# One row of a modulation product moved from TensorE to VectorE, and the first loads of a decoder layer put in another order

## The chip, the cores and the metric

The kernel runs on one core of a Trainium2 chip. The metric is the device time of one execution in microseconds (us). Beside the time of every run there is one profiled execution of the kernel before, and all rows below come from it.

A core has five engines that work side by side: TensorE (PE, matrix products; its weight loads are listed as PEld), VectorE (DVE), ScalarE (ACT), GpSimd (POOL) and SyncE (SP, which here only issues DMA transfers). Each engine runs its own instructions in a fixed order and waits on semaphores of the others. ACT can issue transfers too.

## The reference, cut to what matters

The reference is one decoder layer on 256 tokens of width 2048. A vector `c` gives six modulation rows; the rest is a norm, a mixer of three head groups, a residual add, a second norm, a mixture of 32 experts, and a last norm:

```
mod = (silu(c) @ ada_w + ada_b)[:, None, :]
sh1, sc1, g1, sh2, sc2, g2 = jnp.split(mod, 6, axis=-1)
h = rmsnorm(x, norm1_g) * (1.0 + sc1) + sh1
x = x + g1 * hybrid_mixer(h, w_in, conv_w, a_log, dt_bias, dn_norm_g, sinks, w_out)
h = rmsnorm(x, norm2_g) * (1.0 + sc2) + sh2
x = x + g2 * hierarchical_moe(h, rg_w, rg_b, re_w, re_b, w_gate, w_up, w_down)
return rmsnorm(x, final_norm_g)
```

`ada_w` is 2048 x 12288. Each of the six rows is a product of one vector of 2048 with a 2048 x 2048 block, so each costs 16 tiles of 128 x 2048 (1 MB each). All is float32; the large products split a number into two float32r parts.

## The kernel before, in words

Weights pass through ring slots of 128 x 2048 floats (1 MB). A `Stream` holds the queue of loads; `st.grow(...)` hands it slots, `pump()` issues a load for each free slot on SP's queue, and `done()` frees a slot once its tile was used. The first 90 tiles come from `early`: slices of sh1 and sc1 (`ada_tile`, the tiles named `prow`), slices of the input projection, then paired columns of it and the output projection `w_out`. The other four rows come from `ada_w`, 64 tiles: g1 (i = 0), sh2 (1), sc2 (2) and g2 (3). After that come the experts.

At the start the kernel reads `c`, `x` (four tiles `xt`, 512 KB each), six small pieces of norm1_g and ada_b (`crow`), and `w_bb` (`wbr`). It squares x on ACT (`ssq`, then `rs`, a square root, a reciprocal), spreads the result over the columns (`rd`, `rb`), turns the modulation of the first 256 columns into `mod` (`modulate`), and forms the normed, modulated input `hx` (`input_rows`), with which the projections `w` start. This is repeated for each of six slices of the 2048 columns.

`split` cuts a weight tile into a high part (a cast on ACT) and a low part (a subtraction, on VectorE or on GpSimd by turns); its tiles are `stg`.

`row_tile(i, kt)` takes tile kt of row i of `ada_w`. There are two forms. `on_pe` issues four TensorE matmuls (32 x 512) per tile that add up in PSUM (`prow`). `on_dve` keeps a 128 x 2048 sum `racc` in SBUF: two VectorE instructions per tile (128 x 1024 each: a multiplication for kt = 0, a multiply-add after that), and at kt = 15 four matmuls with the column `onec`, which add the partitions of `racc` up. Before, only i = 2 (sc2) took `on_dve`.

The mixer runs the DeltaNet (`delta`) on many short steps between TensorE and VectorE: `vtok`, `Um`, `ktok`, `Sm`, `ob`, `qk`. Between its steps `tick()` puts tiles of the attention groups, of the remaining input projection and of the rows. Then `wout_part` does the output projection in 4 parts and a second round of 4: products into two PSUM banks `w` from a ring of three, then on VectorE a multiplication with g1 (`g1s`) and an addition to x1. Behind each of the first four parts stand two g2 tiles (kt = 8 to 15); kt = 0 to 7 stand in `fill` before.

The order on each engine is not the program's order alone: the kernel is built with a scheduler that places instructions by a model of their durations, so an edit can move instructions elsewhere. A transfer takes one of eight semaphores in turn, over all queues together; the issue waits until the transfer that had that semaphore before has landed.

## Time and profile before

| what | value |
|---|---|
| median of 3 runs | 1624.28 us (1623.28 to 1625.85) |
| the profiled execution's own time | 1624.69 us |
| its span in the profile | 1622.9 us |
| mean granted TensorE clock | 0.98 |
| busy: PE, PEld | 1521.0 us (94%), 926.3 us (57%) |
| busy: DVE, ACT, POOL | 732.8 us (45%), 400.4 us (25%), 184.0 us (11%) |

The span is the time from the first to the last recorded instruction; the 1.8 us between it and the time lie around it. Busy times are sums over the whole span, and the span has stages with different limits, so the table alone doesn't say what an edit is worth.

### The profile page before, as it was taken

Reading aid. Unit: us, or ns where it says so; the run is one execution under the profiler, and the core shown is the slowest. Engines: PE = TensorE matmul, PEld = TensorE weight load, DVE = VectorE, ACT = ScalarE, POOL = GpSimd, SP = SyncE. Lnnn points to the kernel's source line nnn. Section 1 sums busy time; section 2 is a strip of 40 time slices with the busy share of each in tenths; the row PEclk is TensorE's granted clock in tenths of the full one; section 3 lists DMA queues with packets and bytes.
Section 4 is the critical chain, followed back from the end, with each engine's and each line's share of the span. In section 5 each row is a group of like instructions: output and inputs, shape, how many; then the busy total and the mean of one; then the engine's idle time right before and its main releaser. Section 6 shows DMA issues by size and latency. Waiting matters only on the chain. (4 is left out here: it accounts for less than half of the span.)

```text
span 1622.9 us, 23431 instructions
## 1 busy us (share of the span) xinstructions
PE 1521.0 (94%) x9852; PEld 926.3 (57%) x9852; DVE 732.8 (45%) x1201; ACT 400.4 (25%) x691; POOL 184.0 (11%) x103
## 2 busy tenths in 40 slices
PE   5999999999999999899999999999999999999895
PEld 3778877678776677445445445455445435445433
DVE  3544587487624544333443443344235225325325
ACT  4333366444443344120110110111011101101103
POOL 1111223234333241000000000000000000000001
PEclk8999999999999999899999999999999999999998
DMA  9977654888857374799999999999999999999995
GB/s 377 408 300 290 216 224 178 349 316 320 312 216 291 144 305 180 281 410 420 392 420 420 421 421 420 421 420 420 420 421 421 420 421 421 421 420 420 422 420 223
DMA packets 81412, 573.74 MB, mean 354 GB/s; under 512 B 9740, under 2 KB 10100, under 8 KB 12312
## 3 DMA queue, kind: packets, MB, share of 16 engines
q1 hardware_dynamic: 81272, 572.20, 87.4%
q8 instruction: 79, 1.29, 0.3%
q14 instruction: 29, 0.24, 0.0%
q10 hardware_dynamic: 32, 0.01, 0.0%
HBM read 570.07 MB, written 2.10 MB: 353 GB/s over the span
## 5 line engine op out<-in xcount | busy, mean ns | idle before, releaser
L67 PE MATMUL u<-ring,xg 128*64 128x512 f32 x2048 | 483.7, 602 | 7.5 <-DMA ring<-in_expert_gu_dram 7.3
L67 PEld LDWEIGHTS u<-ring,xg 128*64 128x64 f32 x2048 | 134.4, 136 | 235.7 <-issue 190.7
L67 PE MATMUL d<-ring,hidT 128*64 128x256 f32 x2048 | 239.1, 384 | 12.0 <-DMA ring<-in_expert_dn_dram 8.6
L67 PE MATMUL w<-hx,stg 128*128 128x256 f32 x1440 | 191.0, 288 | 7.4 <-ACT hx L349 2.8
L67 PEld LDWEIGHTS d<-ring,hidT 128*64 128x64 f32 x2048 | 144.1, 137 | 93.1 <-issue 10.6
L67 PEld LDWEIGHTS w<-hx,stg 128*128 128x128 f32 x1440 | 177.9, 191 | 32.8 <-issue 10.9
L290 POOL TENSOR_TENSOR stg<-ring,stg 128x1024 fp32r<-128x1024 f32 x50 | 121.9, 2439 | 373.0 <-ACT stg L289 273.4
L289 ACT CAST stg<-ring 128x1024 fp32r<-128x1024 f32 x116 | 121.3, 1047 | 164.3 <-PE w L67 140.9
L1248 DVE TENSOR_TENSOR xt<-xt,s 128x512 f32<-128x512 f32 x120 | 82.5, 687 | 159.2 <-PE s L67 158.4
L1235 ACT CAST yh<-z 64x512 fp32r<-64x512 f32 (+1 forms) x132 | 78.8, 597 | 279.2 <-DVE z L1232 274.3
L1232 DVE SCALAR_TENSOR_TENSOR z<-d,gs,g2b 64x512 f32<-64x512 f32 (+1 forms) x132 | 95.8, 726 | 84.0 <-PE d L67 81.8
L290 DVE TENSOR_TENSOR stg<-ring,stg 128x1024 fp32r<-128x1024 f32 x66 | 91.4, 1385 | 65.2 <-ACT stg L289 65.0
L67 PE MATMUL prow<-ring,csil 128*32 128x512 f32 (+1 forms) x768 | 102.3, 565 | 13.8 <-DMA ring<-in_early_dram 13.5
L1337 POOL TENSOR_TENSOR xf<-xt,fgb 128x1024 f32<-128x1024 f32 x3 | 7.0, 2359 | 953.1 <-DVE xf L1232 953.1
L1165 DVE TENSOR_TENSOR xg<-g,sh2c 128x512 f32<-128x512 f32 x64 | 43.6, 690 | 136.8 <-PE u L67 76.2
L67 PEld LDWEIGHTS s<-yh,wt 128*128 128x128 f32 x240 | 45.4, 189 | 96.4 <-issue 60.4
L1204 ACT ACTIVATE hid<-u 64x512 f32<-64x512 f32 x32 | 18.9, 590 | 317.4 <-PE u L67 300.8
L1236 DVE TENSOR_TENSOR yl<-z,yh 64x512 fp32r<-64x512 f32 (+1 forms) x132 | 87.3, 661 | 5.1 <-ACT yh L1235 1.5
L67 PE MATMUL s<-yh,wt 128*128 128x256 f32 x240 | 75.6, 335 | 9.1 <-ACT yh L1235 5.0
L67 PE MATMUL w<-stg,hx 128*128 128x256 f32 x576 | 81.1, 291 | 0.7 <-DVE ak L271 0.7
L1205 DVE TENSOR_TENSOR hid<-hid,u 64x512 f32<-64x512 f32 x32 | 22.1, 690 | 129.8 <-ACT hid L1204 129.6
L67 PEld LDWEIGHTS w<-stg,hx 128*128 128x128 f32 x576 | 71.1, 189 | 13.2 <-issue 9.8
(396 smaller groups left out, 1590.4 us busy)
## 6 DMA issues: line engine op xcount, KB each, us to landing
ring<-in_expert_gu_dram SPq DMA_DIRECT2D x256, 1024.0 KB, 19.8
ring<-in_expert_dn_dram SPq DMA_DIRECT2D x128, 1024.0 KB, 19.8
ring<-in_early_dram SPq DMA_DIRECT2D x90, 1024.0 KB, 8.2
ring<-in_ada_w_dram SPq DMA_DIRECT2D x64, 1024.0 KB, 6.4
xt<-in_x_dram SPq DMA_DIRECT2D x8, 512.0 KB
out_dram<-xt SPq DMA_DIRECT2D x8, 256.0 KB, 3.9
fgb<-in_final_norm_g_dram SPq DMA_DIRECT2D x1, 1024.0 KB
rw<-in_router_w_dram SPq DMA_DIRECT2D x1, 320.0 KB, 5.1
```

What stands on the lines that cost most here:

```text
L67: return T.matmul(o, lhsT, rhs, start=start, stop=stop, skip_group_check=True)
L289: S.copy(hi, src)
L290: (G if nsplit[0] % GS[part] == GS[part] - 1 else V).tensor_tensor(lo, src, hi, op=ALU.subtract)
L1165: V.tensor_tensor(self.xg[:, 2 * q:2 * q + 2, 0:w], p[:, 0:2 * w].rearrange("p (k s) -> p k s", k=2), sh2c.rearrange("p n k -> p (n k)")[: ...
L1204: S.activation(hid[64:128], p[0:64], AF.Silu)
L1205: V.tensor_tensor(hid[0:64], hid[64:128], p[64:128], op=ALU.mult)
L1232: V.scalar_tensor_tensor(o.rearrange("p (n j) -> p n j", n=m), pd[q, 0:256 * m].rearrange("p (n j) -> p n j", n=m), gs[q, h, u:u + 1], g2h ...
L1235: S.copy(ys[h][q, c], o)
L1236: V.tensor_tensor(yl[h][q, c], o, ys[h][q, c], op=ALU.subtract)
L1248: V.tensor_tensor(x1[n][:, b], x1[n][:, b], p, op=ALU.add)
L1337: G.tensor_tensor(xf[n // 2][:, n % 2], x1[n], fgb[:, None, 512 * n:512 * (n + 1)].to_broadcast([P, NB, 512]), op=ALU.mult)
```

## The change

The g2 row (i = 3) takes `on_dve` as the sc2 row does. At the start, `st.grow(main, side)` (five 1 MB tiles of `early`) stands before the four x loads on SP's queue, not behind them; the six small row loads and `w_bb` are issued from ACT's queue and no longer from SP's, the small rows lie in `scratch` buffers (tag `t2`, four of them, which the squares use too), and the cast and the subtraction that make `wbb` stand ahead in the program. The layout of x (128 rows of 4 KB per tile) is the same in both kernels.

```
     cols, crows = {}, {}
     for nk, r in ((4, 4), (2, 8)):
         w = P * nk
-        rows = crows[nk] = tmp.tile([P, 2, 256], F32, name="crow", tag="ct", bufs=2).rearrange("p u t -> p (u t)")[0:3 * r, 0:w]
-        for i, row in enumerate((norm1_g[0, 0:r * w], ada_b[0, 0:r * w], ada_b[0, D:D + r * w])):
-            start_loads.append((rows[i * r:(i + 1) * r], row.rearrange("(j n) -> j n", n=w)))
+        rows = crows[nk] = scratch(w, 3 * r)
+        S.dma_start(rows[0:r], norm1_g[0, 0:r * w].rearrange("(j n) -> j n", n=w))
+        S.dma_start(rows[r:2 * r], ada_b[0, 0:r * w].rearrange("(j n) -> j n", n=w))
+        S.dma_start(rows[2 * r:3 * r], ada_b[0, D:D + r * w].rearrange("(j n) -> j n", n=w))
...
+    st.grow(*main, *side)
     for n in range(4):
         nc.sync.dma_start(x1[n], xin[n])
-    st.grow(*main, *side)
-    wbr = tmp.tile([P, 2, 384], F32, name="wbr", tag="pT").rearrange("p u s -> p (u s)")[:, 0:16 * KT]
-    for a in start_loads + [(wbr, w_bb)]:
-        nc.sync.dma_start(*a)
...
+    wbr = tmp.tile([P, 2, 384], F32, name="wbr", tag="pT").rearrange("p u s -> p (u s)")[:, 0:16 * KT]
+    S.dma_start(wbr, w_bb)
...
+    S.copy(wbb[0], wbr)
+    V.tensor_tensor(wbb[1], wbr, wbb[0], op=ALU.subtract)
...
         def f(t):
-            (on_dve if i == 2 else on_pe)(t)
+            (on_dve if i >= 2 else on_pe)(t)
...
     V.tensor_copy(rb, pt[:, 0:256])
-    S.copy(wbb[0], wbr)
-    V.tensor_tensor(wbb[1], wbr, wbb[0], op=ALU.subtract)
     use(first[3:CP])
```

How the order moves, at three places. First the start, on TensorE. `prow` are the products of the modulation slices (four 1 MB tiles are 32 matmuls), `d<-ident` are transposes of the small rows and of x, `t_225`/`t_227` is the scaled identity that carries the root of the squares, `t_244` and `t_248` are the copies of `prow` for sh1 and sc1, and `w` are the projections. Before:

```order
L180 MATMUL d<-ident,t_104 128x16
L67 MATMUL prow<-ring,csil 32x256 x40
L233 MATMUL d<-ident,crow 128x12 x4
L233 MATMUL d<-ident,crow 128x24 x2
L67 MATMUL d<-t_225,ones 128x128 x2
L67 MATMUL d<-ones,t_244 128x1 x2
L67 MATMUL d<-ones,t_248 128x1 x2
L334 MATMUL d<-ident,xt_66 128x128 x4
L67 MATMUL prow<-ring,csil 32x256 x8
L67 MATMUL w<-hx,stg 128x256 x48
L67 MATMUL prow<-ring,csil 32x256 x8
```

The same place on TensorE in the changed kernel:

```order
L181 MATMUL d<-ident,t_110 128x16
L67 MATMUL prow<-ring,csil 32x256 x32
L232 MATMUL d<-ident,t_101 128x12 x4
L232 MATMUL d<-ident,t_105 128x24 x2
L67 MATMUL d<-t_227,ones 128x128
L67 MATMUL d<-ones,t_244 128x1 x2
L337 MATMUL d<-ident,xt_66 128x128 x4
L67 MATMUL prow<-ring,csil 32x256 x6
L67 MATMUL d<-t_227,ones 128x128
L67 MATMUL d<-ones,t_248 128x1 x2
L67 MATMUL prow<-ring,csil 32x256 x10
L67 MATMUL w<-hx,stg 128x256 x36
```

One tile's eight `prow` matmuls moved from before the small transposes to behind those of x, and sixteen stand directly ahead of `w`. On ACT's queue the order at the start is now this (before, `c` alone was issued there, the squares L518 stood directly behind its activation, and the cast of `wbr` stood behind the two copies of `prow`):

```order
L241 DMA wbr<-in_w_bb_dram 128x256
L168 DMA t_99<-in_c_dram 16x128
L174 DMA t_101<-in_norm_g_dram 4x512
L175 DMA t_101<-in_ada_b_dram 4x512
L176 DMA t_101<-in_ada_b_dram 4x512
L174 DMA t_105<-in_norm_g_dram 8x256
L175 DMA t_105<-in_ada_b_dram 8x256
L176 DMA t_105<-in_ada_b_dram 8x256
L294 ACT_TABLE_LOAD
L294 CAST wbb_149<-wbr 128x256
L179 ACT_TABLE_LOAD
L179 ACTIVATE t_110<-t_99 16x128
```

The activation of `c`, on which all `prow` matmuls depend, now stands behind eight issues, a cast and a second table load.

Second, the hand-over from the second to the third slice, on TensorE (`t_881` is the copy of the last modulation row, whose four columns `d<-ones,t_881` go to VectorE for `mod`). Before:

```order
L67 MATMUL w<-hx,stg 128x256 x22
L67 MATMUL d<-ones,t_881 128x1 x4
L67 MATMUL prow<-ring,csil 32x512 x4
L67 MATMUL w<-hx,stg 128x256 x2
L67 MATMUL w<-hx,wbb_151 16x256
```

In the changed kernel:

```order
L67 MATMUL w<-hx,stg 128x256 x32
L67 MATMUL d<-ones,t_881 128x1 x3
L67 MATMUL w<-hx,stg 128x256 x12
L67 MATMUL d<-ones,t_881 128x1
L67 MATMUL prow<-ring,csil 32x512 x8
L67 MATMUL w<-hx,stg 128x256 x2
L67 MATMUL w<-hx,wbb_149 16x256
```

Behind the last `d<-ones` now stand eight `prow` matmuls, where there were four.

Third, VectorE between the end of the DeltaNet and the output projection. Before, in the second half of the DeltaNet's last unit (L907 to L909 and L914 feed TensorE, L925 adds `ob`):

```order
L914 TENSOR_TENSOR t_4993<-d,beta 128x512
L925 TENSOR_TENSOR ob<-ob,d 128x512
L907 TENSOR_TENSOR t_5007<-d,egc 128x512
L909 TENSOR_TENSOR ob<-d,egc 128x512
L908 TENSOR_TENSOR t_5007<-vtok,t_5007 128x512
L914 TENSOR_TENSOR t_5016<-d,beta 128x512
```

In the changed kernel:

```order
L915 TENSOR_TENSOR t_4977<-d,beta 128x512
L444 SCALAR_TENSOR_TENSOR racc<-ring,csil,racc 128x1024 x2
L926 TENSOR_TENSOR ob<-ob,d 128x512
L444 SCALAR_TENSOR_TENSOR racc<-ring,csil,racc 128x1024
L908 TENSOR_TENSOR t_4991<-d,egc 128x512
L444 SCALAR_TENSOR_TENSOR racc<-ring,csil,racc 128x1024
L910 TENSOR_TENSOR ob<-d,egc 128x512
L909 TENSOR_TENSOR t_4991<-vtok,t_4991 128x512
L915 TENSOR_TENSOR t_5000<-d,beta 128x512
```

Four `racc` instructions stand between the steps of the chain; twenty others stand ahead of this place, behind sc2's last product. And in the second and third part of the output projection (L975/L976 multiply the PSUM bank `w`, L976/L977 add it to x1), before:

```order
L975 TENSOR_TENSOR w<-w,g1s 128x512 x2
L976 TENSOR_TENSOR xt_5025<-xt_5025,w 128x512 x2
L290 TENSOR_TENSOR stg<-ring,stg 128x1024 x2
L975 TENSOR_TENSOR w<-w,g1s 128x512 x2
L976 TENSOR_TENSOR xt_5026<-xt_5026,w 128x512 x2
L290 TENSOR_TENSOR stg<-ring,stg 128x1024
```

In the changed kernel:

```order
L976 TENSOR_TENSOR w<-w,g1s 128x512 x2
L444 SCALAR_TENSOR_TENSOR racc<-ring,csil,racc 128x1024
L291 TENSOR_TENSOR stg<-ring,stg 128x1024
L444 SCALAR_TENSOR_TENSOR racc<-ring,csil,racc 128x1024
L977 TENSOR_TENSOR xt_5009<-xt_5009,w 128x512 x2
L291 TENSOR_TENSOR stg<-ring,stg 128x1024
L976 TENSOR_TENSOR w<-w,g1s 128x512
L444 SCALAR_TENSOR_TENSOR racc<-ring,csil,racc 128x1024 x2
L976 TENSOR_TENSOR w<-w,g1s 128x512
L977 TENSOR_TENSOR xt_5010<-xt_5010,w 128x512
```

The multiplication and the addition that free a PSUM bank are no longer neighbours. The remaining `racc` instructions stand in front of the first and behind the last of these rows.

## Rows read from the trace of the kernel before

**Rows 1.** The busy time of each engine in two stretches of the span (start:end, length, then busy us and count for PE, PEld, DVE, ACT and POOL, the granted TensorE clock as a share of full speed, the share of the DMA engines, GB/s).

```profile
0.00:690.00 690.00, 644.21 (x4558) 494.44 (x4559) 369.95 (x611) 280.58 (x486) 177.03 (x100) 0.97 0.72 277
690.00:1600.00 910.00, 869.91 (x5252) 427.44 (x5251) 350.97 (x568) 111.58 (x188) 0.00 (x0) 0.99 1.01 418
```

**Rows 2.** The timeline of the first 45 us (start, us, engine, line, operation, out<-in, shapes and count; in brackets the idle time before it and what ended it).

```profile
0.76 1.82 SPq L221 DMA_DIRECT2D xt<-in_x_dram  x4
...
9.27 0.19 ACT L518 ACTIVATION_READ_ACCUMULATOR t<-xt 128x1 f32 x1
...
10.64 1.94 PE L67 MATMUL prow<-ring,csil 128*32 128x256 f32 x16 [6.69 <-DMA ring<-in_early_dram]
...
11.21 0.48 DVE L526 TENSOR_SCALAR t<-ident,rs 128x128 f32<-128x128 f32 x2
...
18.01 1.94 PE L67 MATMUL prow<-ring,csil 128*32 128x256 f32 x16 [0.56 <-DMA ring<-in_early_dram]
...
24.08 0.63 PE L334 MATMUL d<-ident,xt 128*128 128x128 f32 x4
29.24 1.94 PE L67 MATMUL prow<-ring,csil 128*32 128x256 f32 x16 [4.53 <-DMA ring<-in_early_dram]
31.24 7.86 PE L67 MATMUL w<-hx,stg 128*128 128x256 f32 x48
...
40.72 4.47 PE L67 MATMUL w<-hx,stg 128*128 128x256 f32 x38
```

**Rows 3.** Busy times, granted clock and transfer rate of a short stretch at the start, columns as in rows 1.

```profile
30.00:40.00 10.00, 9.94 (x76) 8.27 (x68) 8.10 (x22) 4.45 (x7) 1.39 (x6) 0.72 1.02 428
```

**Rows 4.** The timeline at the hand-over from the second to the third slice, columns as in rows 2.

```profile
86.44 1.07 PE L67 MATMUL prow<-ring,csil 128*32 128x512 f32 x8
...
86.83 2.34 POOL L290 TENSOR_TENSOR stg<-ring,stg 128x1024 fp32r<-128x1024 f32 x1 [9.36 <-ACT stg L289]
86.89 2.30 DVE L324 SCALAR_TENSOR_TENSOR mod<-mod,cols 128x4 f32<-128x4 f32 x1
...
90.31 0.80 PE L67 MATMUL w<-hx,stg 128*128 128x256 f32 x2 [2.79 <-ACT hx L349]
...
91.24 1.94 PE L67 MATMUL prow<-ring,csil 128*32 128x512 f32 x8
```

**Rows 5.** The row matmuls on TensorE from 440 to 600 us: the two groups (count, ns min/median/max, first and last start), and a row of their timeline. A 512-wide matmul leaves two records, so eight are one tile; 128 of the 136 start after sc2's `racc,onec` and are g2's 16 tiles.

```profile
L67 PE MATMUL prow<-ring,csil x136: 592/592/617, 440.8 to 567.4; 128*32 128x512 f32 x136
L67 PE MATMUL prow<-racc,onec x8: 592/605/617, 455.6 to 456.0; 128*32 128x512 f32 x8
...
564.72 1.91 PE L67 MATMUL prow<-ring,csil 128*32 128x512 f32 x12
```

**Rows 6.** sc2's row on VectorE (tile `racc`): durations in ns, first and last start, and, from the groups of VectorE's lines in 310 to 437 us, the busy us and the mean.

```profile
L441 DVE SCALAR_TENSOR_TENSOR racc<-ring,csil,racc x30: 1255/1276/3402, 317.2 to 432.9; 128x1024 f32<-128x1024 f32 x30
L439 DVE TENSOR_SCALAR racc<-ring,csil x2: 741/741/741, 312.2 to 312.8; 128x1024 f32<-128x1024 f32 x2
...
L441 DVE SCALAR_TENSOR_TENSOR racc<-ring,csil,racc 128x1024 f32<-128x1024 f32 x30 | 42.4, 1453 | 4.1 <-DMA ring<-in_ada_w_dram 4.1
```

**Rows 7.** Busy times by stretch, columns as in rows 1: where sc2's row is on VectorE (310 to 437, and ten microseconds of it in which VectorE has no gap), and from sc2's last product to the end of the DeltaNet.

```profile
310.00:437.00 127.00, 122.20 (x999) 103.28 (x998) 98.29 (x135) 53.82 (x120) 49.94 (x28) 1.00 0.84 319
320.00:330.00 10.00, 7.72 (x60) 5.65 (x56) 9.92 (x15) 2.06 (x4) 4.04 (x2) 1.00 0.90 326
...
456.60:510.00 53.40, 53.40 (x397) 40.69 (x395) 18.59 (x29) 22.80 (x44) 19.10 (x9) 1.00 0.73 276
510.00:527.60 17.60, 15.39 (x96) 9.57 (x94) 7.84 (x11) 2.81 (x4) 4.44 (x4) 1.00 0.75 284
```

**Rows 8.** The timeline of VectorE and GpSimd where both work on SBUF, and the same VectorE line a little later.

```profile
495.43 2.40 POOL L938 TENSOR_TENSOR tok<-tok,dng 128x1024 f32<-128x1024 f32 x1
...
496.22 2.15 DVE L917 TENSOR_TENSOR t<-t,ekd 128x512 f32<-128x512 f32 x1
...
506.00 0.69 DVE L917 TENSOR_TENSOR t<-t,ekd 128x512 f32<-128x512 f32 x1
```

**Rows 9.** The timeline of TensorE and VectorE at the end of the DeltaNet.

```profile
514.49 2.78 PE L67 MATMUL prow<-ring,csil 128*32 128x512 f32 x22
...
519.26 0.69 DVE L914 TENSOR_TENSOR t<-d,beta 128x512 f32<-128x512 f32 x1 [0.20 <-PE d L67]
...
522.82 1.06 PE L67 MATMUL prow<-ring,csil 128*32 128x512 f32 x8
...
524.53 1.13 PE L67 MATMUL d<-t,Um 128*128 128x128 f32 x8 [0.64 <-DVE t L908]
...
525.69 0.69 DVE L914 TENSOR_TENSOR t<-d,beta 128x512 f32<-128x512 f32 x1 [1.31 <-PE d L67]
```

**Rows 10.** The timeline of the output projection around its first and second part.

```profile
547.62 1.40 DVE L975 TENSOR_TENSOR w<-w,g1s 128x512 f32<-128x512 f32 x2 [2.51 <-PE w L67]
...
548.82 1.92 PE L67 MATMUL prow<-ring,csil 128*32 128x512 f32 x16 [0.30 <-DMA ring<-in_ada_w_dram]
548.92 1.27 DVE L976 TENSOR_TENSOR xt<-xt,w 128x512 f32<-128x512 f32 x2
...
550.12 1.22 DVE L290 TENSOR_TENSOR stg<-ring,stg 128x1024 fp32r<-128x1024 f32 x1
...
551.94 0.86 PE L67 MATMUL w<-stg,aq 128*128 128x512 f32 x3
```

More of the change, by code (lines that the diff above doesn't have):

```diff
@@ L168, in hybrid_moe @@
     S.dma_start(craw, c[0].rearrange("(k p) -> k p", p=P))
-    cols, crows, start_loads = {}, {}, []
+    cols, crows = {}, {}
     for nk, r in ((4, 4), (2, 8)):
         w = P * nk
-        rows = crows[nk] = tmp.tile([P, 2, 256], F32, name="crow", tag="ct", bufs=2).rearrange("p u t -> p (u t)")[0:3 * r, 0:w]
-        for i, row in enumerate((norm1_g[0, 0:r * w], ada_b[0, 0:r * w], ada_b[0, D:D + r * w])):
-            start_loads.append((rows[i * r:(i + 1) * r], row.rearrange("(j n) -> j n", n=w)))
+        rows = crows[nk] = scratch(w, 3 * r)
+        S.dma_start(rows[0:r], norm1_g[0, 0:r * w].rearrange("(j n) -> j n", n=w))
+        S.dma_start(rows[r:2 * r], ada_b[0, 0:r * w].rearrange("(j n) -> j n", n=w))
+        S.dma_start(rows[2 * r:3 * r], ada_b[0, D:D + r * w].rearrange("(j n) -> j n", n=w))
     V.memset(csil, 0.0)
```

## The prediction

> **What bounds the kernel now.** I read the profile in this order: busy times by stretch, the waits of TensorE, then the timelines of the two regions that the change touches, and last the chain of instructions on VectorE there. The busy times [rows 1] split the span in two. From 690 us on, the DMA engines move 418 GB/s without a gap (share 1.01): the experts' weights set the pace there, and nothing of this change lies in that stretch. Up to 690 us the DMA share is 0.72 and TensorE is busy 644 of 690 us, VectorE 370: there TensorE is the bound. The expert loads follow on as ring slots come free, so a microsecond won before about 680 us should shift the whole rest by a microsecond. The change has to be worth what it takes from TensorE's line before that point, less what TensorE then waits for.
>
> **The start.** Before, x (2 MB) goes first, and the five early tiles behind it arrive 2.46 us apart (TensorE takes the first at 10.64, the fourth at 18.01) [rows 2]. With the tiles ahead of x, the first lands about 2 x 2.46 = 4.9 us earlier, at 5.7, and the fifth at 15.6; the x tiles of half a megabyte then land from 17 to 20.8. Two things follow.
>
> The squares, which ended at 9.46 before, now wait for x: two squares of 0.8 us behind the last x tile end at 22.4. From the last square to the end of the scaled identity took 11.69 - 9.27 = 2.4 us [rows 2], so it is ready at about 24.8, where before it was ready at 11.7 and waited for TensorE. Meanwhile the activation of `c` waits behind eight issues on ACT, one of which waits for the semaphore of the first early tile; with two table loads and the cast I put `csil` at 11, and four tiles of products at 1.94 us end at 18.8. They are not last; `csil` could be 5 us later without a cost. TensorE is then idle for some 6 us to 24.8, where before it was idle 4.53 us to 29.24 [rows 2].
>
> From there the second half of the spread, the modulation, the normed columns and `hx` follow. The like of it ran from the transposes of x (24.08 to 24.71) to 31.24 before [rows 2], 6.5 us, so I put the first `w` at 31.5 instead of 31.24: no gain. But before, TensorE came to `w` out of its wait at half clock: 48 matmuls took 7.86 us, 38 later ones 4.47 (0.118 each), and the granted clock of 30 to 40 us was 0.72 [rows 2, 3]. In the new order sixteen `prow` matmuls (fifth and sixth tile, both landed) stand ahead of `w`, and I take the 48 at 0.118: 5.7 us. The end of this group moves from about 40.1 to 38.2: **1.9 us gained**. If the clock rises later, little is left (0.5); if the chain to `hx` is shorter because GpSimd is elsewhere, 3.
>
> **The hand-over at 87 us.** Before, TensorE did four matmuls (1.07 us, eight records) behind the last modulation column, then was idle for 2.79 us until `hx`, and ran the next ones at half clock (1.94 for eight records) [rows 4]. On the way a VectorE instruction of 128 x 4 took 2.30 us beside a GpSimd subtraction that began 0.06 us earlier. Eight matmuls stand there now: one microsecond more cover, and as the wait shortens some of the half clock goes too. **2.0 us gained**; 0 if the schedule around it shifts the gap elsewhere, 4.6 if wait and half clock both go. The other reorderings up to 130 us move work between engines that show no wait of TensorE there; I cost them at nothing, since the ring is full and TensorE's queue covers them (where a new gap opened, it would be of this size, 1 to 3 us).
>
> **g2 off TensorE.** The 128 records are 16 tiles. A tile alone shows 1.07 us [rows 4], one and a half in a row 1.91 [rows 5]; at the middle of 1.07 and 1.27, some 1.19 each, they are 19.0 us of TensorE in all. By their places in the timeline 9.6 of it lies in 459 to 493, 4.7 in 510 to 524, 4.7 behind 548. On VectorE they become 2 instructions of 0.74 and 30 of 1.28 at the median, 1.45 at the mean with what GpSimd blocks [rows 6], 40 to 45 us, and two pieces of `onec` products come back to TensorE (1.0 us each by a tile's price).
>
> 456 to 510 us: TensorE has no gap there, VectorE is busy 18.6 us of 53.4 [rows 7]. The new order puts 20 `racc` instructions in: 2 x 0.74 + 18 x 1.28 = 24.5, or 27.6 at the mean. That makes 43 to 46 us of VectorE work, and TensorE's share falls to 53.4 - 9.6 = 43.8. So VectorE becomes as full as TensorE. Where sc2's row did this before, VectorE at 77% (98.3 of 127) went with 4.8 us of 127 lost by TensorE, but ten microseconds without a gap on VectorE (9.92) with 2.28 of 10 [rows 7]. Between these, at some 15% of 44 us, TensorE loses 6.6 of its 9.6: **3.0 us gained**, bounds 0 and 9.6.
>
> 510 to 528 us: the new order puts two plus one plus one `racc` instructions between steps of the chain that leads to the last `qk` product. From L914 at 519.26 to L914 at 525.69 took 6.4 us [rows 9]. In the new order that is about 0.6 + 2 x 1.28 + 0.6 + 1.28 + 0.6 + 1.28 + 0.6 + 0.7 + 1.0 (TensorE's product between) = 9.2: 2.8 us more, and nothing is left for TensorE in this time. Ahead of it the `prow` pieces of 510 and 514 go (3.7 us), of which some 2.9 was not needed to cover the chain. **0**, bounds -3 and +2.
>
> 548 to 568 us: 4.7 us of `prow` go. But in the second part L976 now follows L975 behind two `racc` and a split: 1.40 + 1.28 + 1.22 + 1.28 + 0.64 = 5.8 us until the first PSUM bank is free, where TensorE has twelve matmuls of some 0.24 us as cover (2.8) [rows 10]: 3.0 us idle at most. In the third part two `racc` (2.6 us) stand inside the pair, against a cover of some seven: about 2 us. With the `onec` pieces (2.0) that is 7.0 against 4.7: **2 us lost** (bounds -5 and +1).
>
> The sum is 1.9 + 2.0 + 3.0 + 0 - 2.0 = 4.9 us gained. Of the profiled execution's 1624.69 us that leaves 1619.8; the median of before is 0.4 lower than that execution, so I give 1619.4.
>
> **Two instructions on one memory.** The rows show that a VectorE instruction with two SBUF inputs is held while GpSimd works: L917 took 2.15 us beside a GpSimd instruction, 0.69 alone [rows 8]. The Trainium skill (SBUF — State Buffer, "Who interferes with whom") speaks against this change: VectorE and GpSimd share a pair of ports under an exclusive lock, and a VectorE instruction with two SBUF inputs and a GpSimd one that reads SBUF hold each other off for the whole instruction. The trace agrees, and each `racc` multiply-add is of that kind. By the rule, with GpSimd busy 19.1 of 53.4 us [rows 7], VectorE would have 43 + 19 = 62 us of work there if all of it collided, and the gain of that stretch would turn into a loss of 8; the mean of 1.45 against 1.28 says that in sc2's stretch only about a seventh was lost. So I price the rule as the far end of rival C.
>
> **The rivals.**
>
> A, the forecast above: chance 0.43, its own range 1614 to 1624.
>
> B, VectorE hides g2 altogether: TensorE has the matmuls no more and nothing else waits. Then 19.0 - 2.0 = 17.0 with the 3.9 of the first two places: 1624.7 - 20.9 - 0.4 = 1603.4. For it: VectorE's 45% and 370 of 690 us [rows 1]. Against it: the ten full microseconds of rows 7 and the written order. Chance 0.12.
>
> C, slower: `racc` ahead of the chain's and the output projection's steps. In 456 to 510 nothing is won; at the end of the DeltaNet the 2.8 us longer chain and two locks of 1.46 us (2.15 - 0.69) cost 5.8, the output projection 3.3 and two locks more, 6.2. With 3.9 won at the start, that is 8.1 lost: 1624.7 + 8.1 - 0.4 = 1632.4. It decides as soon as these stretches lose more than 7.2 us together. For it: the order on VectorE is fixed, and TensorE has no filler left between these steps. Against it: GpSimd is busy only 4.4 of 17.6 us there [rows 7]. Chance 0.20.
>
> D, nothing is won at the start and the hand-over: the wait for the squares takes the place of the wait for the tiles, and half clock stays. Then only 3.0 + 0 - 2.0 is left: 1623.3. For it: x is 16 us later, and TensorE's new idle time (6 us) is longer than the old one (4.53). Chance 0.25.
>
> **How the numbers follow.** A measurement of this kernel can tell some 0.2% from no change, 3.25 us: faster is below 1621.0, slower above 1627.5. B and four fifths of A are faster (0.12 + 0.34), and a sliver of D: 0.47. Same is the rest of A and most of D: 0.30. Slower is C and a little of D where a new gap opens at the start: 0.23. The range leaves B out (0.12) and the far half of C: 1608 to 1631.
>
> **What would show it.** Right: first `w` near 31 us at full clock; the idle time at the hand-over under 2 us; VectorE over 90% busy from 456 to 505 with TensorE short of full; TensorE waits for `t` and for `w` banks released by VectorE between 505 and 570. Wrong: first `w` clearly behind 33 us, or a wait of `prow` for `csil` behind 16 us (the start); TensorE without gaps from 456 to 570 (B); waits there of over 15 us (C).

## The result, and the profile after

The changed kernel takes 1633.49 us (median of 6 runs, 1630.71 to 1634.44); the kernel before took 1624.53 us beside it (6 runs). The ratio is 1.0051 (95%: 1.0041 to 1.0061): **slower by 0.5%**, where 1619.4 was forecast. The profiled execution took 1630.71 us, its span 1628.9. It is the fastest of the six, and its span is 6.0 us longer than that of before: the rows below account for 6.0 of the 8.3 us that the ratio gives.

The windows of the changed kernel, columns as in rows 1, answer to [rows 1, 3, 7]:

```profile
0.00:690.00 690.00, 626.10 (x4401) 495.11 (x4401) 409.56 (x642) 281.06 (x487) 179.36 (x100) 0.95 0.71 273
690.00:1600.00 910.00, 872.47 (x5245) 427.96 (x5244) 346.81 (x559) 107.09 (x178) 0.00 (x0) 0.99 1.01 418
456.60:510.00 53.40, 46.70 (x312) 41.06 (x311) 46.27 (x46) 22.60 (x44) 20.71 (x8) 0.90 0.80 315
510.00:527.60 17.60, 9.80 (x53) 8.26 (x53) 12.84 (x15) 1.17 (x2) 3.16 (x3) 0.80 0.52 180
30.00:40.00 10.00, 9.91 (x97) 8.19 (x90) 9.72 (x29) 4.90 (x8) 1.14 (x4) 1.00 1.01 420
```

TensorE has 18 us less to do up to 690 us, and is not done sooner: its idle time grew from 45.8 to 63.9 us, and its granted clock fell from 0.97 to 0.95. From 690 us on the two are nearly alike.

**Where the time went.** One and the same instruction is looked up in both timelines, and its start before is taken from its start after. Four places do: sc2's product on TensorE (455.6 before [rows 5]), the last two `t<-d,beta` of the DeltaNet (519.26 and 525.69 [rows 9]), and the last multiplication with g1, at 642.00 before:

```profile
642.00 1.39 DVE L975 TENSOR_TENSOR w<-w,g1s 128x512 f32<-128x512 f32 x2 [6.15 <-PE w L67]
```

In the changed kernel (the second of the four rows is that of 519.26 before):

```profile
451.98 1.07 PE L67 MATMUL prow<-racc,onec 128*32 128x512 f32 x8
514.51 0.69 DVE L915 TENSOR_TENSOR t<-d,beta 128x512 f32<-128x512 f32 x1 [0.71 <-PE d L67]
525.73 0.69 DVE L915 TENSOR_TENSOR t<-d,beta 128x512 f32<-128x512 f32 x1 [2.23 <-PE d L67]
648.84 1.39 DVE L976 TENSOR_TENSOR w<-w,g1s 128x512 f32<-128x512 f32 x2 [6.15 <-PE w L67]
```

So the changed kernel is 3.57 us ahead at 456, 4.75 ahead at 519, level at 526, and 6.84 behind at 642. These four shifts, called s1 to s4, are given for every experiment below. Only e2 and e3 have none: the executions that were profiled, 1928.53 and 1747.44 us, ran at a lower clock throughout, and the ratios leave them out.

The timeline at the start, at the hand-over, at one wait of TensorE in between, and at TensorE's waits in the chain and in the output projection, there with what stands ahead of them on VectorE:

```profile
24.89 0.80 PE L67 MATMUL d<-t,ones 128*128 128x128 f32 x2 [7.00 <-DVE t L529]
31.35 4.67 PE L67 MATMUL w<-hx,stg 128*128 128x256 f32 x36
...
86.32 0.17 DVE L327 SCALAR_TENSOR_TENSOR mod<-mod,cols 128x4 f32<-128x4 f32 x1
86.59 2.37 POOL L291 TENSOR_TENSOR stg<-ring,stg 128x1024 fp32r<-128x1024 f32 x1 [10.33 <-ACT stg L290]
89.29 0.74 PE L67 MATMUL w<-hx,stg 128*128 128x256 f32 x4 [1.07 <-DVE hx L353]
...
476.38 2.07 PE L67 MATMUL w<-stg,hx 128*128 128x256 f32 x8 [2.02 <-DVE stg L291]
...
515.12 3.59 DVE L444 SCALAR_TENSOR_TENSOR racc<-ring,csil,racc 128x1024 f32<-128x1024 f32 x2
516.55 1.08 POOL L943 TENSOR_TENSOR t<-ob 128x512 f32<-128x512 f32 x1 [0.90 <-PE d L67]
519.24 1.27 DVE L444 SCALAR_TENSOR_TENSOR racc<-ring,csil,racc 128x1024 f32<-128x1024 f32 x1
521.03 1.27 DVE L444 SCALAR_TENSOR_TENSOR racc<-ring,csil,racc 128x1024 f32<-128x1024 f32 x1
522.83 0.67 DVE L909 TENSOR_TENSOR t<-vtok,t 128x512 f32<-128x512 f32 x1
523.65 2.05 PE L67 MATMUL d<-t,Um 128*128 128x128 f32 x8 [5.50 <-DVE t L909]
...
542.41 2.16 DVE L291 TENSOR_TENSOR stg<-ring,stg 128x1024 fp32r<-128x1024 f32 x1 [2.17 <-ACT stg L290]
544.63 7.59 SPq L190 DMA_DIRECT2D ring<-in_ada_w_dram  x2
549.38 2.48 DVE L444 SCALAR_TENSOR_TENSOR racc<-ring,csil,racc 128x1024 f32<-128x1024 f32 x2 [3.62 <-DMA ring<-in_ada_w_dram]
551.78 1.29 DVE L976 TENSOR_TENSOR w<-w,g1s 128x512 f32<-128x512 f32 x2
554.17 1.22 DVE L291 TENSOR_TENSOR stg<-ring,stg 128x1024 fp32r<-128x1024 f32 x1
555.44 0.80 PE L67 MATMUL w<-stg,aq 128*128 128x512 f32 x1 [4.23 <-DVE stg L291]
573.36 0.73 PE L67 MATMUL w<-stg,aq 128*128 128x512 f32 x2 [1.96 <-DVE xt L977]
```

Three things are to be read here. At 523.65 the eight products of the chain have waited 5.50 us, where they waited 0.64 before [rows 9], and then take 2.05 us where they took 1.13. At 549.38 VectorE, with a g2 tile at the head of its queue, stands still for 3.62 us until that tile has landed; the split of 554.17 is queued behind, and TensorE, which needs it at 551.2, waits 4.23 us. Before, TensorE took a g2 tile at nearly the same time (548.82) and waited 0.30 [rows 10].

The tile could not land sooner. SP's queue had stood for 21.9 us until the end of VectorE's split of 542.41 freed a ring slot; the tile's load went out at 544.63 (the row holds two loads, this is the first), and VectorE could go on 4.75 us later. Before, the same load went out at 543.97. So the change did not make this tile late; it changed who waits for it.

And behind such waits the granted clock falls; 0.50 is its lower level, 1.2 GHz. Behind 476.38 and behind 555.44, in short windows:

```profile
475.00:480.00 5.00, 3.62 (x17) 3.62 (x18) 5.00 (x8) 2.49 (x11) 0.00 (x0) 0.60 0.73 249
480.00:485.00 5.00, 5.00 (x41) 4.63 (x40) 4.05 (x6) 3.60 (x6) 3.45 (x1) 0.71 0.97 381
...
555.00:560.00 5.00, 4.56 (x11) 3.59 (x12) 2.78 (x4) 0.00 (x0) 0.00 (x0) 0.50 0.85 306
```

### The profile page after: what moved, and what is told of

It reads as the page before. It is cut to its first block, busy times and chain, and to the rows that moved or that the text cites. A ratio compares the mean times of both kernels' runs of the same rounds, so it can differ in the third digit from the quotient of the medians.

```text
span 1628.9 us, 23242 instructions
## 1 busy us (share of the span) xinstructions
PE 1510.4 (93%) x9732; PEld 930.9 (57%) x9732; DVE 772.8 (47%) x1233; ACT 400.9 (25%) x692; POOL 186.3 (11%) x103
## 3 DMA queue, kind: packets, MB, share of 16 engines
q8 instruction: 78, 1.28, 0.3%
## 5 line engine op out<-in xcount | busy, mean ns | idle before, releaser
L444 DVE SCALAR_TENSOR_TENSOR racc<-ring,csil,racc 128x1024 f32<-128x1024 f32 x60 | 86.6, 1475 | 7.0 <-DMA ring<-in_ada_w_dram 7.0
L67 PE MATMUL w<-stg,hx 128*128 128x256 f32 x576 | 84.5, 299 | 2.9 <-DVE stg L291 2.0
L67 PEld LDWEIGHTS w<-stg,hx 128*128 128x128 f32 x576 | 74.6, 198 | 13.5 <-issue 8.3
```

Source lines behind the costliest of these rows:

```text
L67: return T.matmul(o, lhsT, rhs, start=start, stop=stop, skip_group_check=True)
L444: V.scalar_tensor_tensor(acc[:, c], t[:, c], csil[:, kt, 3:4], acc[:, c], op0=ALU.mult, op1=ALU.add)
```

## The experiments

Every ratio is to the kernel before, run in turn on the same chip; e13 is a single run. "Start" means the changed order of the first loads with all that belongs to it.

| label | what it is | median us | ratio (95%) | s1 | s2 | s3 | s4 |
|---|---|---|---|---|---|---|---|
| after | start, all of g2 on VectorE | 1633.49 | 1.0051 (1.0041 to 1.0061) | -3.57 | -4.75 | +0.04 | +6.84 |
| e1_start | start alone | 1621.16 | 0.9979 (0.9971 to 0.9988) | -2.86 | -2.86 | -2.85 | -3.52 |
| e2_g2 | g2 alone | 1637.0 | 1.0073 (1.0060 to 1.0086) | | | | |
| e9_xfirst | e1, x ahead of the five tiles | 1619.81 | 0.9970 (0.9959 to 0.9981) | -3.84 | -3.84 | -3.83 | -4.56 |
| e3_g2_first8 | start, tiles 0 to 7 on VectorE | 1621.54 | 0.9979 (0.9969 to 0.9990) | | | | |
| e13_first8_again | the same once more | 1623.2 | (one run) | -1.06 | -3.39 | -2.37 | -2.43 |
| e4_g2_last8 | start, tiles 8 to 15 on VectorE | 1634.4 | 1.0059 (1.0046 to 1.0072) | -1.62 | -4.73 | +0.02 | +9.75 |
| e5_chain | start, tiles 8 to 11 on VectorE | 1626.34 | 1.0010 (1.0001 to 1.0019) | -3.34 | -6.45 | -1.71 | +0.25 |
| e6_wout | start, tiles 12 to 15 on VectorE | 1632.31 | 1.0048 (1.0034 to 1.0062) | -1.39 | -1.39 | -1.38 | +8.86 |
| e7_pinned | after, tiles 8 to 15 in program order | 1633.52 | 1.0045 (1.0032 to 1.0059) | -1.41 | -3.28 | -3.27 | +11.93 |
| e12_pinned_no_pool | e7, no GpSimd splits in the output projection | 1628.4 | 1.0018 (1.0009 to 1.0027) | -2.49 | -3.84 | -3.83 | +3.82 |
| e10a_tiles | e6, tiles 12 to 15 one part later | 1623.22 | 0.9983 (0.9974 to 0.9992) | -1.12 | -1.12 | -1.11 | -0.49 |
| e10b_resident | e10a, data already in SBUF | 1622.01 | 0.9977 (0.9968 to 0.9986) | -2.48 | -2.49 | -2.48 | -2.69 |
| e14_resident_early | e6's place, data already in SBUF | 1616.71 | 0.9945 (0.9931 to 0.9958) | -0.75 | -0.76 | -0.74 | -1.68 |
| e15_swapped | e6, the g2 tiles loaded and used first | 1627.29 | 1.0013 (1.0004 to 1.0022) | -1.70 | -1.70 | -0.57 | +2.18 |
| e16_xfirst_swapped | e15, x ahead of the five tiles | 1625.82 | 1.0002 (0.9993 to 1.0011) | -4.31 | -4.31 | -3.17 | -0.45 |

e13 repeats e3 for its trace. s1 holds the start, and differs by up to 2.8 us between kernels whose start is the same, so of the other parts the steps from s1 on are read.

### The two halves of the change: e1_start, e2_g2

My theory after the result: the start wins, g2 on VectorE loses. e1 takes back g2, e2 takes back the start.

```
-            (on_dve if i >= 2 else on_pe)(t)
+            (on_dve if i == 2 else on_pe)(t)
```

> The start's edits alone; g2 stays on TensorE as before. Theory (the loss is g2's row between the steps of the DeltaNet and of the output projection; the start is a gain): the 4.5 us that the trace of the changed kernel is ahead at 300 us stay to the end, about 1620 us against 1624.5. Rival (the start is paid back later, by the ring or by the experts' loads): 1623 to 1625.

> g2 on VectorE alone; the start as before. Theory: the changed kernel without its 4.5 us at the start, 1635 to 1638 us. Rival (start and g2 don't simply add, because the new start is what makes g2's tiles late): 1624 to 1630.

The theory holds, and both times fall into their ranges: e1 is 0.2% faster (some 3.4 us), e2 0.7% slower (some 11.9). Their sum, 8.5 us slower, is the change (8.3).

### Which tiles lose: e3_g2_first8, e4_g2_last8, e5_chain, e6_wout, e13_first8_again

A list says which tiles of g2 VectorE takes; the rest stays on TensorE and adds into the same PSUM bank, and the `onec` matmuls follow as the last part of the sum.

```
+        here = [k for k in range(KT) if i == 2 or (i == 3 and (k < 8))]    # e3, e13
+        # e4: k >= 8      e5: 8 <= k < 12      e6: k >= 12
-            (on_dve if i >= 2 else on_pe)(t)
+            (on_dve if kt in here else on_pe)(t)
```

> The changed kernel, but only g2's tiles 0 to 7 go to VectorE; tiles 8 to 15 stay on TensorE, and the sum on VectorE is folded into the same PSUM bank at the end. No VectorE instruction of g2 stands then among the last steps of the DeltaNet or in the output projection. Theory (those places are where the loss arises): both losses go, 5.2 and some 6.8 us, and the stretch from 456 to 500 keeps its gain: 1616 to 1621 us. Rival (VectorE, full from 456 to 500 and locked against GpSimd, is the loss): 1626 to 1633.

> The opposite: tiles 0 to 7 of g2 on TensorE, 8 to 15 on VectorE, where two tiles stand among the last steps of the DeltaNet and four in the output projection. Theory: the loss of some 5 us at the end of the DeltaNet and some 6 in the output projection stays, less 4.5 at the start: 1628 to 1634 us. Rival (the fullness of VectorE from 456 to 500 is the loss): 1619 to 1623.

> The changed kernel with only g2's tiles 8 to 11 on VectorE, the others on TensorE: the four multiply-adds between the last steps of the DeltaNet stand as in the changed kernel, none stands in the output projection. Theory (the chain at the end of the DeltaNet costs some 5 us by itself, whatever g2 does elsewhere): the start alone (1621.2) plus 4 to 6, so 1625 to 1627 us. Rival (the longer chain only takes up waits that the output projection had anyway): 1620 to 1622.

> The changed kernel with only g2's tiles 12 to 15 on VectorE: they stand among the multiplications and additions of the output projection's second and third part, and VectorE waits there for the tiles' transfers. Theory (a multiply-add that waits for its tile holds up the split and the bank behind it; 5 to 8 us): the start alone (1621.2) plus 5 to 8, so 1626 to 1629 us. Rival (the order alone, without the wait for the transfer, costs 2): 1622 to 1624.

> The kernel with g2's tiles 0 to 7 on VectorE once more, for a profile of the stretch from 456 to 510 us. Theory (VectorE is so full there that TensorE waits for the splits as long as the eight tiles took): the end of the stretch is at most 2 us ahead of the start alone. Rival (the time is won there and lost behind): 5 us or more ahead at 510 us.

The loss lies in tiles 8 to 15. Tiles 8 to 11 alone (e5) cost 5 us over e1, tiles 12 to 15 alone (e6) 11, which is 3 more than I expected for them. Together (e4) they cost 13, less than the two added. Tiles 0 to 7 (e3) win nothing over e1, though they take 9.6 us off TensorE: in e13 their stretch shows

```profile
456.60:510.00 53.40, 47.23 (x344) 39.85 (x343) 41.95 (x44) 22.59 (x44) 21.67 (x9) 0.97 0.75 295
```

6.2 us without work on TensorE, and VectorE busy 42 us; 2.3 us are won up to s2, and 1.0 of it is gone at s3. In e5 the shape of the chain's loss is that of the changed kernel, on VectorE and TensorE:

```profile
513.42 3.55 DVE L447 SCALAR_TENSOR_TENSOR racc<-ring,csil,racc 128x1024 f32<-128x1024 f32 x2
...
521.90 2.04 PE L67 MATMUL d<-t,Um 128*128 128x128 f32 x8 [5.46 <-DVE t L918]
```

3.1 us are won up to s2 (the four tiles' matmuls), then 4.7 are lost between s2 and s3, as in e4 (4.75) and in the changed kernel (4.8). The other 2 us of e5 go behind s3, most of them to the `onec` products (1.9 us from 566.02 on). e6 loses nothing up to s3 and 10.2 us behind it. On VectorE and, below, among the waits of TensorE from 540 to 600 us (us in total, times, longest):

```profile
546.63 1.42 DVE L445 TENSOR_SCALAR racc<-ring,csil 128x1024 f32<-128x1024 f32 x2 [3.58 <-DMA ring<-in_ada_w_dram]
566.93 2.48 DVE L447 SCALAR_TENSOR_TENSOR racc<-ring,csil,racc 128x1024 f32<-128x1024 f32 x2 [4.82 <-DMA ring<-in_ada_w_dram]
...
PE w L67 <- DVE stg L291: 4.3, 1, 4.3
PE prow L67 <- DVE racc L447: 3.1, 1, 3.1
```

Twice VectorE stands still for a tile. Both loads had gone out, at 541.92 and 562.19, with the end of a split on VectorE that freed their slot. TensorE and ScalarE wait for no transfer in this trace from 500 to 645 us. Either these waits are the cause, or the places of the `racc` instructions among the output projection's steps are, tile or no tile.

### Order, or late tiles: e7_pinned, e12_pinned_no_pool

My theory at this point was the order that the scheduler chose. e7 keeps the `racc` instructions of tiles 8 to 15 where the program has them, behind the multiplication and the additions that empty a part's PSUM banks (its evacuation); e12 also takes GpSimd's share of the splits in the output projection away.

```
+                    ins = V.scalar_tensor_tensor(...)
+                    if i == 3 and kt >= 8:
+                        tc.keep_in_program_order(ins)
-GS = (3, 2, 2)
+GS = (3, 2, 1000)     # e12 alone
```

> The changed kernel with all of g2 on VectorE, but the multiply-adds of tiles 8 to 15 are kept in the program's order on VectorE: none stands in the DeltaNet's chain any more, and in the output projection each pair stands behind the multiplication and the additions of a part. Theory (the place on VectorE's queue is the loss, not the work): both losses go and some of TensorE's 19 us is won, 1615 to 1622 us. Rival (VectorE gives ring slots back later than TensorE did, so weights come late wherever the work stands): 1628 to 1636.

> The kernel with all of g2 on VectorE and tiles 8 to 15 in program order, and in the output projection no split on GpSimd: all subtractions there go to VectorE, so nothing of GpSimd holds the multiply-adds. Theory (the lock between VectorE and GpSimd made the loss of the output projection in the pinned kernel, 1633.5): 1620 to 1627 us. Rival (tiles and slots come late, or VectorE is simply full there): 1631 us or more.

The theory fell. The chain's loss is gone in e7 (s3 - s2 = 0), but the output projection loses 15 us in place of 7, and the time is in the rival's range. e12 loses 7.6 there, and its time lies between those of its theory and its rival. Its trace and that of e7 from 450 to 690 us (e7 first):

```profile
450.00:690.00 240.00, 201.08 (x1036) 153.38 (x1035) 153.73 (x198) 82.89 (x136) 66.06 (x30) 0.91 0.58 220
...
450.00:690.00 240.00, 207.66 (x1060) 156.60 (x1060) 156.56 (x214) 82.38 (x134) 20.51 (x14) 0.91 0.61 230
```

GpSimd is busy 45 us less, VectorE 3 us more, and e12 is 5 us faster than e7: five pairs of `racc` took 4.0 to 4.6 us in e7, every pair 2.5 in e12. But a subtraction that took GpSimd 2.4 us takes VectorE 1.2, so the 5 us are not the lock's alone. Even so e12 is slower than e1 by 6 to 7.

### The same order with and without the wait: e10a_tiles, e10b_resident, e14_resident_early

All three put tiles 12 to 15 by hand around the multiplications with g1 (`L976` of the changed kernel): in parts 3 and 4 in e10a and e10b, in parts 2 and 3 in e14, near where the scheduler put them in e6. e10a uses the tiles. e10b and e14 read `ob`, which is in SBUF by then, so the row g2 lacks its last four tiles; the tiles are still loaded, and their slots come free when they land.

```
+    def row_in(n, j):
+        _, _, fn = rows_q[56 + 2 * n + j]       # e14: rows_q[58 + 2 * n + j], n in (1, 2)
+        fn(st.get())                            # e10b, e14: fn(ob_f4[0]...)
...
+        if n in (2, 3) and not q_done[n]:
+            row_in(n, 0)
         for b in range(NB):
-            V.tensor_tensor(acc[b], acc[b], g1s, op=ALU.mult)
+            pin(V.tensor_tensor(acc[b], acc[b], g1s, op=ALU.mult))
+        if n in (2, 3) and not q_done[n]:
+            row_in(n, 1)
...
```

> The start plus g2's tiles 12 to 15 on VectorE, put by hand at a fixed place: one tile's two multiply-adds ahead of the two multiplications with g1, one tile's between these and the two additions, in the third and fourth part of the output projection. It is the twin of the next kernel; VectorE's order is the same in both. Theory (VectorE waits for a tile that lands late, and the work behind it waits too): the start alone (1621.2) plus 5 to 11, 1626 to 1632 us. Rival (the order alone costs): the same time as its twin, within 2 us.

> Its twin: the same instructions of VectorE in the same order, but the multiply-adds of tiles 12 to 15 read the tile ob, which lies in SBUF already, in place of g2's tiles, so g2's last four tiles are left out of the sum; the four tiles are still loaded, and their slots are free as soon as they land. Theory (the wait for the transfers is the loss): 1620 to 1624 us, at least 4 us less than its twin. Rival (order and lock alone): the same as its twin.

> The kernel with tiles 12 to 15 on VectorE at the place where the scheduler put them (second and third part of the output projection, VectorE's order nearly that of the 1632.3 us kernel), but reading the resident tile ob in place of g2's tiles, so g2's last four tiles are left out of the sum; they are still loaded and their slots are free when they land. Theory (at this place VectorE waits for tiles that have not landed, 8.4 us by its waits, and the multiplications, the splits and TensorE wait behind it): the loss goes, 1619 to 1624 us. Rival (the place itself, ahead of a bank's release, is the loss): 1628 us or more.

One part later the tiles have landed: e10a shows no wait of VectorE for a transfer, and loses 0.6 us from s3 to s4, e10b wins 0.2. Neither order nor tiles cost much there: the twins differ by 1.2 us, where I had expected at least 4. e14 is the one that tells: the same instructions at nearly e6's place, with nothing to wait for. VectorE's row beside 566.93 of e6, and TensorE's waits from 540 to 600 us:

```profile
557.73 2.47 DVE L447 SCALAR_TENSOR_TENSOR racc<-ob,csil,racc 128x1024 f32<-128x1024 f32 x2
...
PE w L67 <- POOL stg L291: 2.4, 4, 1.0
PE w L67 <- DVE xt L1000: 1.5, 1, 1.5
```

From s3 to s4 e14 wins 0.9 us where e6 loses 10.2. So 11 us hang on tiles that are not there yet when VectorE comes to them. Two other things differ between e6 and e14: in e14 a slot comes free when its tile lands, and the order is e6's only nearly (the first `racc` pair stands ahead of two other instructions). The slots are no rival up to here, since in e6 nothing but these `racc` waits for a transfer. The order by itself costs these 3.9 us of waits (0.9 in e1) and a piece of `onec` products of 1.75, about what four tiles save on TensorE (4.7): without late tiles the move wins 0.3 us over e1 in this stretch (e1 wins 0.7 from s3 to s4).

e14's time must not be read as a gain from that step. Its span is 8.0 us shorter than before, its s4 only 1.7. The rest is won behind it: from 642 to 700 us the loads run with a share of 0.86 against 0.80 in e1, and TensorE takes 26 expert products in a row at 667.56 where it took 16 at 668.45 in e1. It may be that the scheduler's order of the first expert products frees slots sooner there; that was not tested.

### Loading and using them first: e15_swapped, e16_xfirst_swapped

If late tiles are the cause, the g2 tiles of the last two parts can be loaded ahead of the output projection's own.

```
-        for _, load, _ in on(st, w_items[2 * n:2 * n + 2]) + rows_q[56 + 2 * n:58 + 2 * n]:
+        pair = (on(st, w_items[2 * n:2 * n + 2]), rows_q[56 + 2 * n:58 + 2 * n])
+        for _, load, _ in [x for part in (pair if n < 2 else pair[::-1]) for x in part]:
...
+        if n >= 2:
+            use(rows_q[56 + 2 * n:58 + 2 * n])
         wout_part(...)
-        use(rows_q[56 + 2 * n:58 + 2 * n])
+        if n < 2:
+            use(rows_q[56 + 2 * n:58 + 2 * n])
```

> The kernel with g2's tiles 12 to 15 on VectorE, but in the last two pairs the loads of g2's tiles stand ahead of the output projection's, and their use too; the scheduler then puts the multiply-adds ahead of the output projection. All of the work is done. Theory (a tile that lands in time makes the place harmless): the loss of 11 us goes, 1617 to 1624 us. Rival (the slots that g2's tiles hold make the output projection's tiles late in their stead): 1626 us or more.

> The same, with x ahead of the five early tiles as in the kernel of 1619.8 us. If both gains add, 1616 to 1621 us; if the former kernel is slow, this one is slow by as much less 1 to 2.

Better than e6 by 5 us, and not the gain I hoped for. The scheduler now puts the `racc` among the last steps of the DeltaNet and its norm (522 to 536 us), and the loss is there: 1.1 us up to s3, and on TensorE, from 515 to 600 us, where the like wait in e1 was 1.9,

```profile
PE w L67 <- DVE t L470: 4.3, 1, 4.3
```

e16 is e15 with x first, and 1.5 us better, as e9 is against e1.

### What wins at the start: e9_xfirst

```
-    st.grow(*main, *side)
     for n in range(4):
         nc.sync.dma_start(x1[n], xin[n])
+    st.grow(*main, *side)
-            (on_dve if i >= 2 else on_pe)(t)
+            (on_dve if i == 2 else on_pe)(t)
```

> The start alone (g2 on TensorE), but x goes ahead of the five early tiles again, as before the change; the small loads stay on ACT's queue. Theory (the gain at the start comes from the small loads leaving SP's queue; the tiles ahead of x only move TensorE's wait from the tiles to the squares, 6 to 7 us idle): the squares are done early, the first projections start near 25 us instead of 31, and 3 to 7 us are won over the start alone: 1614 to 1618 us. Rival (the order of x and tiles is what wins): the time of before, 1623 to 1625, or the same as the start alone if the transfers set the pace (1620 to 1622).

With x first again, and the small loads on ACT's queue as in the change, nothing is lost against e1. Its start on TensorE:

```profile
27.80 1.94 PE L67 MATMUL prow<-ring,csil 128*32 128x256 f32 x16 [3.33 <-DMA ring<-in_early_dram]
30.00 5.85 PE L67 MATMUL w<-hx,stg 128*128 128x256 f32 x36 [0.27 <-ACT hx L352]
```

`w` starts 1.24 us sooner than before, and its first 36 matmuls take 5.85 us at a granted clock of 0.85 (30 to 40 us); in e1 they start at 31.81 and take 4.67 at 1.00. The two ways come out nearly alike (the intervals overlap); the 3 to 7 us over e1 that I expected did not come. So the gain is not in the order of x and the tiles. What e1 and e9 share is that the seven small loads no longer stand in SP's queue (with their new buffers and the earlier `wbb`, which were not split off). Before, these seven stood there between the fifth load of `early` and the next eleven, which went out from 20.52 us on; in e9 the sixteen follow one another from 4.75 on. In the first 30 us the DMA engines move 385 GB/s in e9 and 386 in e1, where they moved 359 before. e9, with g2 left on TensorE, is faster than both kernels by the median, 0.3% (0.19 to 0.41) against before.

## Why the prediction was wrong, step by step

By the shifts, the sum in the changed kernel is 3.6 - 1.9 - 1.7 - 6.8 = -6.8 us, where 3.9 + 3.0 + 0 - 2.0 = 4.9 was forecast. (The 3.1 us of `prow` pieces ahead of the chain lie before s2; they are counted with the chain, as in the forecast.) Two steps failed most: what the slow clock behind a wait costs, for which the sum had terms at the start and the hand-over and none in the three places behind, and the arrival of the tiles.

**The start and the hand-over, 3.9 us: right in sum, the parts in part by luck.** The two together came to 3.6 us at s1 in the changed kernel and 3.4 by e1's times. `w` starts at 31.35 (31.5 forecast), the granted clock of 30 to 40 us is 1.00 (0.72 before), and TensorE's idle time for the scaled identity is 7.00 (6 forecast). But at the hand-over only 0.6 of the start's 1.9 us is left: L327 stands at 86.32 where it stood at 86.89 [rows 4]. The hand-over then wins 2.1 (`hx` begins at 87.04, 2.7 ahead), and the rest came between 87 us and s1, where nothing was forecast. At the hand-over the wait is 1.07 us, not 2.79; the reason lies less in the eight products that I named than in GpSimd, whose subtraction now begins at 86.59, behind L327, which then takes 0.17 instead of 2.30. One part of the forecast does not stand: that tiles ahead of x are what helps (e9). And the start of this profile is the rarer one: of the twelve kernels with the tiles ahead of x that have a profile to lay beside it, `w` starts at 31.4 to 31.8 in three (after, e1, e5) and at 33.2 to 33.4 in nine, at a granted clock of 0.73 to 0.81 from 30 to 40 us, with s1 from -0.75 to -2.49. There half clock stays, as rival D said, and the first `w` is behind 33 us, the forecast's own sign of a wrong start. D's sum fell by e1's times all the same.

**456 to 510 us, 3.0 us: the first term that failed.** "TensorE loses 6.6 of its 9.6": it is without work for 53.40 - 46.70 = 6.7, and VectorE works 46.27 us, as forecast (43 to 46). Left out was what follows the waits. The granted clock there is 0.90, so of 46.70 busy us some 4.7 are lost, by estimate; behind the wait of 2.02 us at 476 it was 0.60 and then 0.71. With the 3.1 us of pieces that left the queue ahead of the chain, 9.6 + 3.1 - 6.7 - 4.7 = 1.3, and the gain from s1 to s2 is 1.2. Without these pieces the stretch lost some 1.9 us.

**510 to 528 us, "0": 1.7 us too good.** The 2.9 us ahead of the chain came (3.1 in e5). The chain itself grew by 4.8 us, not 2.8. The sum had four `racc` at 1.28; the first two took 3.59 together, 1.0 more, beside GpSimd instructions of which one of 1.08 us lies wholly within. And the products behind the wait ran at half clock, 2.05 instead of 1.13. The Trainium skill (SBUF — State Buffer, "Who interferes with whom") says that a VectorE instruction with two SBUF inputs contends with a GpSimd one that reads SBUF. These two rows agree; what the lock alone costs a whole stretch no run shows.

**Output projection, -2.0: 4.8 us too good.** 6.8 us were lost (s4 - s3). For the second part I wrote 3.0 us idle at most, from the durations of what stands in VectorE's queue up to the release of a PSUM bank. The wait was 4.23, and it was for a split: ahead of the instructions that I added up stands one more pair of `racc`, which stood 3.62 us for its tile and then took 2.48. The next 13 matmuls then took 5.72 us, 0.44 each where the same kind took 0.24 twenty us later: 2.6 us more. The third part's 2 us were right (1.96), and so were the `onec` products (2.1). The missing terms are the arrival of the tile and the half clock. Two rows had shown the first: TensorE's 0.30 us wait for a transfer just there [rows 10], and the 4.1 us that sc2's own `racc` had stood idle for DMA [rows 6]. I read both as small, and did not ask what would stand behind the instruction that waits. e6 against e14 shows that 11 us go with this wait and few with the order that the sum was made of. Added up, the slow clock behind waits (4.7, then 0.9 in the chain, then 2.6) is by this estimate some 8 of the 11.7 us between forecast and profile.

**The rivals.** C (1632.4, 0.20) is nearest in time and in its places: nothing in 456 to 510, 5.8 at the chain, 6.2 in the output projection. Its mechanism was half right: locks stretch the chain, as its price said, but in the output projection there are late tiles and half clock in its place. Its sum is near partly by luck: it has 3.3 for the output projection where the forecast's own terms give 7.0 - 4.7 = 2.3, and leaves out the 2.9 us ahead of the chain; with both it would be 1628.5. Its sign came: TensorE was without work for 22.0 us from 456 to 570 (5.7 before). VectorE was busy 43.1 of 49 us from 456 to 505, just short of the 90% that were to show A. B fell: TensorE's idle time is where the matmuls went.

**What stays open.** Why e12 is still slower than e1 was not split further. Its `racc` pairs run at their own speed, but its trace shows slots that come back late, the rival of e7: SP's queue stands 26.3 us, up to 534.10, until a `racc` frees a slot, and ScalarE's casts (525 to 625 us) then wait for tiles of the output projection, for which they never wait in e1, with TensorE behind one of them:

```profile
ACT stg L290 <- DMA ring<-in_early_dram: 11.6, 3, 7.1
...
562.52 0.99 PE L67 MATMUL w<-stg,aq 128*128 128x512 f32 x2 [2.77 <-ACT stg L290]
```

How much of the 6 to 7 us that is, beside VectorE's fullness, no run tells apart. Nor why e14 and, by less, e10b gain behind s4, nor what makes the start fast in three profiles and slow in nine.

## What to carry to other kernels

Before a piece of work moves from an engine that takes it as filler to one that works in a chain, ask at each new place two things: has its operand landed by then (its load goes out only when some instruction frees a slot), and what is queued behind it. An engine's average idle share answers neither. And price a wait of TensorE with the slow stretch behind it: here a wait of 4.23 us cost another 2.6 in matmuls at half clock.

## What the hardware showed unexpectedly

A lock holds both sides. Two `racc` at 489.10 took 5.12 us, twice their own time, and the GpSimd pair beside them 6.39 where a single one took 2.40 [rows 8]:

```profile
486.75 6.39 POOL L939 TENSOR_TENSOR tok<-tok,dng 128x1024 f32<-128x1024 f32 x2 [1.74 <-ACT tok L938]
489.10 5.12 DVE L444 SCALAR_TENSOR_TENSOR racc<-ring,csil,racc 128x1024 f32<-128x1024 f32 x2
```

And for the same order of loads the start is not the same in every profile: the first `w` stands at 31.35 in the changed kernel, 31.81 in e1, 31.56 in e5, and at 33.2 to 33.4 in the nine others, with the `prow` products ahead of it at 2.77 us in e4 where they took 1.49. That is as large as the gain that was forecast for it.
